# A hybrid sequence-mixing block on one Trainium2 core: the first two SwiGLU tiles in token halves, and the late modulation as one stream

## The chip, the core and the metric

The kernel runs on one core of one Trainium2 chip. A core has a matrix engine (TensorE, PE in the profile; its weight loads are PEld), three engines for element-wise work (VectorE or DVE, ScalarE or ACT, GpSimd or POOL) and SyncE (SP), which here issues transfers. Each engine works through its own instructions in order. An instruction waits at the head of its engine until the semaphores that it needs have been raised, and what stands behind it waits too. Transfers run on 16 DMA engines; they are issued by SP, ACT and POOL.

The metric is the device time of the whole kernel in microseconds (us), from the runs of it, taken as a median. A profile is one execution that the hardware profiler recorded; its times count from the start of its span.

## The reference

One layer of a diffusion backbone on 512 latent tokens (D = 1024) with 256 context tokens in front of them, in float32. The lines that the change touches are these:

```python
m_lat = (jax.nn.silu(c) @ mod_w[layer] + mod_b[layer])[:, None, :]
sh1, sc1, g1, sh2, sc2, g2 = jnp.split(m_lat, 6, axis=-1)
...
def swiglu(h, w_in, w_out):
    gate, up = jnp.split(h @ w_in, 2, axis=-1)
    return (jax.nn.silu(gate) * up) @ w_out
```

The conditioning vector `c` gives six rows of 1024, the modulation: shift, scale and gate of the first norm and mixers, and the same three for the second norm and the SwiGLU. `mod_w` is 1024 x 6144. The first normed and modulated input goes through one projection into two token mixers, a gated delta rule and HGRN2 (each with 4 heads, both directions). Their outputs are gated, projected up, merged and projected to D; times `g1` that is added to the input. The sum `x1` is normed again (RMSNorm, times 1 + `sc2`, plus `sh2`) and goes through the SwiGLU with 2816 features; times `g2` that is added to `x1`, and a last RMSNorm with the weight `final_norm_g` gives the output.

## The kernel before, in words

**Products.** A float32 product is made of three products of float32r operands: each operand is split into a high part and the rest (`hi`, `lo`), and TensorE adds hi.hi, lo.hi and hi.lo in PSUM (`mm3`, L100; the matmul is L105). Weights come through `split` (L84): SP issues the transfer of a 512 KB block `raw` (L92), ScalarE casts it to `hi` (L95), VectorE subtracts to get `lo` (L97). A tile of a pool has a number of buffers; a new tile of the same tag takes the buffer of an old one and waits until the old one's last reader is done. `raw`, `hi` and `lo` have two buffers each in the pool `wf`.

**Order.** The program is written in Python loops, and a scheduler puts each engine's instructions in an order by priority and by what is ready in its estimate; the waits follow from the tiles' readers and writers. So the order on an engine is not simply the order of the code.

**The modulation.** Sections 0 and 1 (first norm) are made at the start. The later sections are made in quarters of 256 columns: a weighted sum over 1024 rows of `mod_w`, in VectorE multiply-adds with the scalar `sc[:, k]`, and a sum over the partitions by two matmuls of one column (`mod_sum`, L843, matmul L846). Seven of the twelve quarters of the sections 2, 3 and 4 are made early, within the delta rule (`mod_early`, L830: transfer of 1 MB into a buffer of the delta rule that is not in use yet, multiplies L837 and L839). The other five (3,3 and 4,0 to 4,3, as section and quarter) are made behind it, and the four of section 5 in the SwiGLU, both by `mod_quarter` (L811): a generator that clears an accumulator (L815), loads half a quarter, 512 KB, by a transfer that GpSimd issues (L819) into one of two buffers, and multiplies it in four steps (L821). One such half is a step; `mods` holds the generators, and `mod_steps(n)` runs n steps. In the trace the halves are all called `mwb`; in the program they have numbers, section, quarter and first row block: `mwb330` is section 3, quarter 3, rows from block 0, `mwb334` its other half. The five quarters behind the delta rule are emitted at once (L915 to L922, ten transfers); those of the SwiGLU come one half to a feature tile, for tiles 3 to 12 (L1056, eight transfers).

**Behind the delta rule** run the rest of the HGRN2 heads (tiles `h_...`: VectorE's L464 and L465, ScalarE's copy L444, TensorE's L448), then merge and up-projection, output projection, and the second norm (L1010 to L1030), which works in two halves of the tokens: TensorE transposes into `px` (L1022), ScalarE and VectorE write the normed input as `hhi` and `hlo` (L1029, L1030). Each of these holds 8 blocks of 128 features by 512 tokens.

**SwiGLU** (L1033 to L1060). For each of 22 feature tiles f: two splits, of the gate's and the up part's weights (L1044); two PSUM banks `pf` (L1045); gate and up products, each 24 matmuls of 128 x 128 by 512 tokens. Tile 0 alone is done in two halves of the tokens, each 2 x 24 matmuls by 256 tokens (L1046), so that it can begin when the first half of the second norm is ready. Then sigmoid on ScalarE (L1051), two products on VectorE (L1052, L1053), and the split of the result into `uh` and `ul` (L1054, L1055). At f = 15 the modulation's section 5 is summed and spread over the partitions into `g2b`. The row `final_norm_g` is loaded to every partition (`fgb`, 512 KB, L1039, by GpSimd) ahead of the loop. The products with `w_out` follow (L1061 onwards), in two halves of the output columns; `g2b` and `fgb` are read behind them.

Of the kernel before, what the change touches and what calls it, by code (L numbers as in the profile page):

```python
# [7 lines left out]
F32 = mybir.dt.float32  # L8
F32R = mybir.dt.float32r
U8 = mybir.dt.uint8  # L10
AF = mybir.ActivationFunctionType
ALU = mybir.AluOpType

P = 128
D = 1024
KT = 8
# [13 lines left out]
# The order in which the streams of the mixers are emitted: name and number of steps; X ends the delta rule.  # L30
# [13 lines left out]
def view(ap, offset, dims):  # L44
    """The tile behind ap, all partitions, with free dimensions given as (step, count)."""
    return bass.AP(ap.tensor, ap.offset + offset, [list(ap.ap[0])] + [list(d) for d in dims])


def body(tc, T, out, tap=None):
# [8 lines left out]
    with ExitStack() as root:  # L58
# [25 lines left out]
        def split(srcs, kt, n, pool=None):  # L84
            """Loads [kt * 128, n] of weights side by side and splits them into two float32r parts."""
            WN[0] += 1
            pool = pool or ring["w"]
            raw = pool.tile([P, kt, n], F32, name=f"raw{WN[0]}", tag="raw", bufs=2)
# [5 lines left out]
            hi = pool.tile([P, kt, n], F32R, name=f"hi{WN[0]}", tag="hi")  # L94
            nc.scalar.copy(hi[:, :, :], raw[:, :, :])  # L95
            lo = pool.tile([P, kt, n], F32R, name=f"lo{WN[0]}", tag="lo")
# [3 lines left out]
        def mm3(ps, a, b, kt, start=True, stop=True):  # L100
            """ps += sum_k a_k^T b_k with a, b as (hi, lo) callables of k."""
# [6 lines left out]
        def feat(w, src, n, name, t0=0, tag="mm"):  # L108
            """[128 features, n tokens from t0] of the projection with the weights w."""
# [22 lines left out]
        def gate_low(i, pool):  # L132
            """The same in two halves of the features, out of its own buffers."""
# [15 lines left out]
        with ExitStack() as st:  # L149
# [4 lines left out]
            # small vectors, one row of 128 to a partition: those of the first norm, then the others  # L154
# [71 lines left out]
            def sigmoid_small(dst, src):  # L226
                """1 / (1 + exp(-src)), for the small tiles."""
# [25 lines left out]
            def modulation(d, s):  # L253
                """Shift and scale columns of feature tile d, for the latents (s = 0) or the context (s = 1)."""
# [12 lines left out]
            def mod_columns(s, d0, d1):  # L267
                """The columns of the feature tiles d0 to d1, with the biases and the weight of the norm."""
# [144 lines left out]
        def head_norm(po, gcol, i, on, y, ss, tag, name, eq=None):  # L413
            """po: [128 tokens, 4, 128] -> normalised, scaled by the channel weight, transposed, spilled as row i of ydram."""
# [396 lines left out]
        def mod_quarter(sec, j):  # L811
# [12 lines left out]
            def finish():  # L824
                mod_sum(sec, j, acc, "mm")
# [291 lines left out]
```

## Time and profile before

| what | value |
| --- | --- |
| three runs | 1109.54, 1112.13, 1111.83 us; median 1111.83 |
| profiled execution: span | 1115.9 us, 4.07 above the median |
| mean granted clock of TensorE | 0.980 |
| delta rule and all before it, 0 to 540 us | TensorE busy 500.05 of 540.00 |
| HGRN2 tail, merge, output projection, second norm, 540 to 735 us | TensorE busy 184.41 of 195.00 |
| SwiGLU, gate and up products, 735 to 911 us | TensorE busy 173.61 of 176.00 |
| `w_out` products and the last norm, 911 us to the end | TensorE busy 195.94 of 204.90 |

The profiled execution's own time is known as its span; no other time of it was taken. A row of a timeline gives the start and the duration in us, the engine, the line of the kernel, the operation, the tile written and the tiles read (their numbers left out), the number of instructions put together in the row and, in brackets, how long the engine stood idle before it and what ended that. Matmuls overlap, so a matmul's duration is longer than the distance to the next; paces are taken from starts.

### The profile page before, as it was taken

The page shows a single profiled execution, that of the slowest core. Times are in us where ns is not written, and L with a number is a line of the kernel's source. Part 1 is how long each engine was busy: PE and PEld are TensorE (multiplying, and loading weights), DVE is VectorE, ACT ScalarE, POOL GpSimd, SP SyncE. Part 2 cuts the span into 40 slices and gives each one's busy share as a digit, 9 for nine tenths or more (in the row PEclk, how much of TensorE's full clock was granted, in tenths as well). Part 3 has the DMA queues.
Part 4 walks back from the last instruction along what each step waited for, and adds up shares of the span by engine and source line. Part 5 has one row for each costly group of instructions (what it writes and reads, how often), then busy time and mean ns, then how long its engine had stood idle before and what let it go on. Part 6 is the DMA issues. An engine that isn't in the chain of part 4 may idle for free.

```text
span 1115.9 us, 15740 instructions
## 1 busy us (share of the span) xinstructions
PE 1054.0 (94%) x6007; PEld 879.1 (79%) x6007; DVE 696.8 (62%) x1365; ACT 560.1 (50%) x1062; POOL 75.8 (7%) x132
## 2 busy tenths in 40 slices
PE   4999999979999999999988999899999999999996
PEld 3787788858897887799777887787888888888785
DVE  5896877679676868866796675586343433422424
ACT  3454568747886765887764743452222222221212
POOL 0010000220001022000201000010000000000000
PEclk9998999989999999999999999999999999999999
DMA  9943322222003213200637853455333332322222
GB/s 303 283 149 109 114 76 57 58 76 57 3 20 114 76 48 86 57 2 11 194 118 227 299 153 123 129 167 159 93 93 94 94 88 80 93 94 94 92 95 94
DMA packets 142720, 122.02 MB, mean 109 GB/s; under 512 B 5534, under 2 KB 118452, under 8 KB 142644
## 3 DMA queue, kind: packets, MB, share of 16 engines
q1 hardware_dynamic: 135907, 100.20, 30.1%
q0 software_dynamic: 4640, 17.30, 4.8%
q10 hardware_dynamic: 2096, 3.50, 1.0%
q8 instruction: 47, 0.77, 0.3%
q14 instruction: 30, 0.24, 0.1%
HBM read 110.51 MB, written 10.49 MB: 108 GB/s over the span
## 4 chain that ended last, share of the span: by engine, by line
PE 57%; DVE 10%; issue 5%; ACT 3%; POOL 2%; DMA 2%; POOLq 0%; ACTq 0%; DVEq 0%
PE pf L105 19%; PE pfo L105 10%; PE pgate L105 4%; PE pup L105 4%; PE pwo L105 3%; PE h_z L105 2%; DMA mwb<-in_mod_w_dram 2%; PE h_pA L477 2%; PE h_zv L105 1%; DVE lo L97 1%; PE p_s_pk L778 1%; PE p_s_pk L787 1%; DVE p_o L683 1%; PE p_s_pk L775 1%; DVE p_Z L685 1%
## 5 line engine op out<-in xcount | busy, mean ns | idle before, releaser
L95 ACT CAST hi<-raw 128x1024 fp32r<-128x1024 f32 (+1 forms) x137 | 135.7, 991 | 307.4 <-PE pf L105 131.2
L97 DVE TENSOR_TENSOR lo<-raw,hi 128x1024 fp32r<-128x1024 f32 (+1 forms) x137 | 157.9, 1152 | 177.5 <-ACT hi L95 176.9
L105 PE MATMUL pf<-hhi,lo 128*128 128x512 f32 (+1 forms) x368 | 142.9, 389 | 2.4 <-DVE lo L97 2.4
L105 PE MATMUL pf<-hlo,hi 128*128 128x512 f32 (+1 forms) x368 | 143.0, 390 | 0.7 <-DVE hlo L1030 0.7
L105 PE MATMUL pf<-hhi,hi 128*128 128x512 f32 (+1 forms) x368 | 142.4, 390 | 0.0
L105 PEld LDWEIGHTS pf<-hhi,lo 128*128 128x128 f32 x368 | 69.8, 190 | 18.5 <-DVE lo L97 3.3
L105 PEld LDWEIGHTS pf<-hlo,hi 128*128 128x128 f32 x368 | 69.7, 190 | 16.5 <-DVE hlo L1030 1.1
L105 PEld LDWEIGHTS pf<-hhi,hi 128*128 128x128 f32 x368 | 69.7, 190 | 15.1
L105 PE MATMUL pfo<-lo,uh 128*128 128x512 f32 x176 | 69.8, 396 | 0.1
L105 PE MATMUL pfo<-hi,ul 128*128 128x512 f32 x176 | 69.5, 395 | 0.0
L105 PE MATMUL pfo<-hi,uh 128*128 128x512 f32 x176 | 68.7, 395 | 0.0
L105 PE MATMUL pgate<-hhi,lo 128*128 128x512 f32 x144 | 60.6, 422 | 6.7 <-DVE lo L97 6.7
L105 PE MATMUL pgate<-hhi,hi 128*128 128x512 f32 x144 | 61.1, 424 | 1.8 <-ACT hi L95 1.8
L105 PE MATMUL pgate<-hlo,hi 128*128 128x512 f32 x144 | 59.8, 416 | 0.0
L1053 DVE TENSOR_TENSOR sg<-sg,pf 128x512 f32<-128x512 f32 x22 | 15.1, 688 | 53.2 <-PE pf L105 53.2
L821 DVE SCALAR_TENSOR_TENSOR acc<-mwb,sc,acc 128x256 f32<-128x256 f32 x72 | 34.3, 482 | 13.0 <-DMA mwb<-in_mod_w_dram 11.7
L261 DVE SCALAR_TENSOR_TENSOR macc<-mw,sc,macc 128x256 f32<-128x256 f32 x96 | 40.0, 479 | 0.0
L105 PEld LDWEIGHTS pfo<-lo,uh 128*128 128x128 f32 x176 | 33.1, 188 | 8.7 <-DVE lo L97 1.0
L105 PEld LDWEIGHTS pgate<-hhi,lo 128*128 128x128 f32 x144 | 28.5, 198 | 14.4 <-DVE lo L97 9.2
L105 PE MATMUL h_z<-hhi,hi 128*128 128x512 f32 x96 | 39.3, 410 | 0.3 <-ACT abT L365 0.3
L105 PE MATMUL h_z<-hlo,hi 128*128 128x512 f32 x96 | 39.4, 411 | 0.0
L105 PEld LDWEIGHTS pfo<-hi,uh 128*128 128x128 f32 x176 | 32.9, 188 | 8.2 <-ACT hi L95 0.6
(422 smaller groups left out, 2566.3 us busy)
## 6 DMA issues: line engine op xcount, KB each, us to landing
raw<-in_ffn_w_in_dram SPq DMA_DIRECT2D x44, 512.0 KB, 3.9
raw<-in_w_in_dram SPq DMA_DIRECT2D x37, 512.0 KB, 3.9
raw<-in_ffn_w_out_dram SPq DMA_DIRECT2D x22, 512.0 KB, 3.5
mwb<-in_mod_w_dram POOLq DMA_DIRECT2D x18, 512.0 KB, 4.9
mw<-in_mod_w_dram SPq DMA_DIRECT2D x16, 512.0 KB, 6.3
mwe<-in_mod_w_dram POOLq DMA_DIRECT2D x7, 1024.0 KB, 6.2
gdram<-gt SPq DMA_DIRECT2D x24, 256.0 KB, 2.4
raw<-in_w_in_dram SPq DMA_DIRECT2D x18, 256.0 KB, 3.0
```

The source lines that it names most:

```text
L95: nc.scalar.copy(hi[:, :, :], raw[:, :, :])
L97: nc.vector.tensor_tensor(lo[:, :, :], raw[:, :, :], hi.bitcast(F32), op=ALU.subtract)
L105: nc.tensor.matmul(ps, a[u](k), b[v](k), start=(start and n == 0), stop=(stop and n == tot - 1))
L261: nc.vector.scalar_tensor_tensor(acc[:, :], mws[d][:, k, :], col, acc[:, :], op0=ALU.mult, op1=ALU.add)
L477: nc.tensor.matmul(pA[:, P * c:P * c + P], kq[:, 0, P * c:P * c + P], kq[:, 1, P * c:P * c + P], start=True, stop=True)
L683: nc.vector.tensor_tensor(ov, Z[:, r + 1:32, r:r + 1].to_broadcast([P, 31 - r, r]), Z[:, r:r + 1, 0:r].to_broadcast([P, 31 - r, r]), op=AL ...
L685: nc.vector.tensor_tensor(Z[:, r + 1:32, 0:r], Z[:, r + 1:32, 0:r], ov, op=ALU.add)
L775: nc.tensor.matmul(pk[:, 0:P], KTt[:, g, :], S[t][:, :], start=True, stop=True)
L778: nc.tensor.matmul(pk[:, P:2 * P], N[:, d, e, g, :], rt[:, :], start=True, stop=True)
L787: nc.tensor.matmul(pk[:, 2 * P:3 * P], kend[:, :], u[:, :], start=True, stop=True)
L821: nc.vector.scalar_tensor_tensor(acc[:, :], mw[:, k - k0, :], sc[:, k:k + 1], acc[:, :], op0=ALU.mult, op1=ALU.add)
L1053: nc.vector.tensor_tensor(sg[:, :], sg[:, :], pgu[1][:, :], op=ALU.mult)
```

## The change

It has three parts.

1. `split` can take its `hi` and `lo` from another pool with a number of buffers given. The weights of tile 0 come from `wf` as before, those of tile 1 get buffers of their own in the pool `ff`. Tiles 0 and 1 are both done in two halves of the tokens, in the order half 0 of tile 0, half 0 of tile 1, half 1 of tile 0, half 1 of tile 1. `g2b` and `fgb` later use these buffers, so the load of `fgb` is emitted behind the two tiles.
2. The late modulation is one generator over all halves of all quarters (`mod_quarters`). It allocates and loads the buffer of step i + 1 before the multiplies of step i.
3. The first multiply of a quarter writes the accumulator (TENSOR_SCALAR, L835) instead of adding to it, and the clearing goes.

The diff, without the comments that it also removes:

```diff
-        def split(srcs, kt, n, pool=None):
+        def split(srcs, kt, n, pool=None, bufs=None):
...
-            raw = pool.tile([P, kt, n], F32, name=f"raw{WN[0]}", tag="raw", bufs=2)
+            raw = (ring["w"] if bufs else pool).tile([P, kt, n], F32, name=f"raw{WN[0]}", tag="raw", bufs=2)
...
-            hi = pool.tile([P, kt, n], F32R, name=f"hi{WN[0]}", tag="hi")
+            hi = pool.tile([P, kt, n], F32R, name=f"hi{WN[0]}", tag="hi", bufs=bufs)
...
-        def mod_quarter(sec, j):
+        def mod_quarters(qs):
             mp = ring["mod"]
-            acc = mp.tile([P, 256], F32, name=f"acc{sec}{j}", tag="acc", bufs=12 if sec < 5 else 4)
-            nc.vector.memset(acc[:, :], 0.0)
-            for k0 in range(0, KT, MK):
-                mw = mp.tile([P, MK, 256], F32, name=f"mwb{sec}{j}{k0}", tag="mw", bufs=2)
-                c0 = D * sec + 256 * j
-                nc.gpsimd.dma_start(mw[:, :, :], T["mod_w"][0, P * k0:P * k0 + MK * P, c0:c0 + 256].rearrange("(k p) f -> p k f", p=P))
+            steps = [(sec, j, k0) for sec, j in qs for k0 in range(0, KT, MK)]
+            tiles = {}
+
+            def load(i):
+                if i < len(steps):
+                    sec, j, k0 = steps[i]
+                    tiles[i] = mp.tile([P, MK, 256], F32, name=f"mwb{sec}{j}{k0}", tag="mw", bufs=2)
+                    c0 = D * sec + 256 * j
+                    nc.gpsimd.dma_start(tiles[i][:, :, :],
+                                        T["mod_w"][0, P * k0:P * k0 + MK * P, c0:c0 + 256].rearrange("(k p) f -> p k f", p=P))
+
+            load(0)
+            for i, (sec, j, k0) in enumerate(steps):
+                load(i + 1)
+                if k0 == 0:
+                    acc = mp.tile([P, 256], F32, name=f"acc{sec}{j}", tag="acc", bufs=12 if sec < 5 else 4)
+                    late.append(lambda sec=sec, j=j, acc=acc: mod_sum(sec, j, acc, "mm"))
+                mw = tiles.pop(i)
                 for k in range(k0, k0 + MK):
-                    nc.vector.scalar_tensor_tensor(acc[:, :], mw[:, k - k0, :], sc[:, k:k + 1], acc[:, :], op0=ALU.mult, op1=ALU.add)
+                    if k == 0:
+                        nc.vector.tensor_scalar_mul(acc[:, :], mw[:, 0, :], sc[:, 0:1])
+                    else:
+                        nc.vector.scalar_tensor_tensor(acc[:, :], mw[:, k - k0, :], sc[:, k:k + 1], acc[:, :], op0=ALU.mult, op1=ALU.add)
                 yield
...
-        mods += [mod_quarter(*q) for q in quarters]
+        mods.append(mod_quarters(quarters))
...
-            g2b = ff.tile([P, D], F32, name="g2b", bufs=1)
-            fgb = ff.tile([P, D], F32, name="fgb", bufs=1)
-            nc.gpsimd.dma_start(fgb[:, :], T["final_norm_g"].unsqueeze(0).to_broadcast([P, D]))
...
-            mods += [mod_quarter(5, j) for j in range(4)]
+            mods.append(mod_quarters([(5, j) for j in range(4)]))
+            pgus = {}
+
+            def ffn_in(f, wss, t0, n):
+                if f not in pgus:
+                    pgus[f] = [bank(("mm", "ha")[f % 2], f"pf{f}_{j}") for j in range(2)]
+                for j in range(2):
+                    mm3(pgus[f][j][:, t0:t0 + n], [lambda k, t=t: t[:, k, :] for t in wss[j]],
+                        [lambda k, t=t: t[:, k, t0:t0 + n] for t in lat], KT)
+
+            def ffn_weights(f, **kw):
+                return [split([W[:, o + P * f:o + P * f + P]], KT, P, **kw) for o in (0, DFF)]
+
+            w01 = ffn_weights(0), ffn_weights(1, pool=ff, bufs=2)
+            for t0 in (0, 256):
+                for f in range(2):
+                    ffn_in(f, w01[f], t0, 256)
+            g2b = ff.tile([P, D], F32, name="g2b", tag="hi", bufs=2)
+            fgb = ff.tile([P, D], F32, name="fgb", tag="lo", bufs=2)
+            nc.gpsimd.dma_start(fgb[:, :], T["final_norm_g"].unsqueeze(0).to_broadcast([P, D]))
             for f in range(NF):
-                ws = [split([W[:, o + P * f:o + P * f + P]], KT, P) for o in (0, DFF)]
-                pgu = [bank(("mm", "ha")[f % 2], f"pf{f}_{j}") for j in range(2)]
-                for t0, n in ((0, 256), (256, 256)) if f == 0 else ((0, SEQ),):
-                    for j in range(2):
-                        mm3(pgu[j][:, t0:t0 + n], [lambda k, t=t: t[:, k, :] for t in ws[j]],
-                            [lambda k, t=t: t[:, k, t0:t0 + n] for t in lat], KT)
+                if f > 1:
+                    ffn_in(f, ffn_weights(f), 0, SEQ)
+                pgu = pgus[f]
```

In the orders below, `hi` and `lo` carry the number of the weight block: 74 and 75 are gate and up part of tile 0, 76 and 77 of tile 1, 80 and 81 of tile 3. `pf1_0` is the gate bank of tile 1, `pf0_1` the up bank of tile 0, and so on; the number behind the last underscore only tells one buffer from another.

TensorE at the end of tile 0, before:

```order
L105 MATMUL pf0_1_7080<-hhi_73,hi75_7075 128x256
L105 MATMUL pf0_1_7080<-hlo_74,hi75_7075 128x256
L105 MATMUL pf0_1_7080<-hhi_73,lo75_7077 128x256
L105 MATMUL pf1_0_7195<-hhi_73,hi76_7185 128x512
L105 MATMUL pf1_0_7195<-hlo_74,hi76_7185 128x512
L105 MATMUL pf1_0_7195<-hhi_73,lo76_7187 128x512
```

TensorE at the same place, after:

```order
L105 MATMUL pf1_0_7133<-hhi_73,hi76_7073 128x256
L105 MATMUL pf1_0_7133<-hlo_74,hi76_7073 128x256
L105 MATMUL pf0_1_7084<-hlo_74,hi75_7067 128x256
L105 MATMUL pf0_1_7084<-hhi_73,lo75_7069 128x256
L105 MATMUL pf0_1_7084<-hhi_73,hi75_7067 128x256
L105 MATMUL pf0_1_7084<-hlo_74,hi75_7067 128x256
L105 MATMUL pf0_1_7084<-hhi_73,lo75_7069 128x256
L105 MATMUL pf1_1_7134<-hhi_73,hi77_7079 128x256
L105 MATMUL pf1_1_7134<-hlo_74,hi77_7079 128x256
L105 MATMUL pf1_0_7133<-hhi_73,lo76_7075 128x256
```

Tile 1 now comes in matmuls of 256 tokens. Apart from the first two of its gate, all of them stand behind tile 0, the second token half of tile 0 included: the scheduler has not kept the interleaving of the code.

VectorE between the gate's and the up part's split of tile 3, before:

```order
L97 TENSOR_TENSOR lo80_7323<-raw80_7319,hi80_7321 128x1024
L1052 TENSOR_TENSOR sg2_7313<-sg2_7313,pf2_0_7263 128x512
L821 SCALAR_TENSOR_TENSOR acc52_7687<-mwb524_7763,sc_173,acc52_7687 128x256 x4
L821 SCALAR_TENSOR_TENSOR acc53_7837<-mwb530_7839,sc_173,acc53_7837 128x256
L1053 TENSOR_TENSOR sg2_7313<-sg2_7313,pf2_1_7264 128x512
L821 SCALAR_TENSOR_TENSOR acc53_7837<-mwb530_7839,sc_173,acc53_7837 128x256
L97 TENSOR_TENSOR lo81_7329<-raw81_7325,hi81_7327 128x1024
```

VectorE at the same place, after:

```order
L97 TENSOR_TENSOR lo80_7366<-raw80_7362,hi80_7364 128x1024
L1076 TENSOR_TENSOR sg2_7356<-sg2_7356,pf2_0_7306 128x512
L837 SCALAR_TENSOR_TENSOR acc52_7732<-mwb524_7730,sc_173,acc52_7732 128x256 x3
L835 TENSOR_SCALAR acc53_7881<-mwb530_7805,sc_173 128x256
L837 SCALAR_TENSOR_TENSOR acc52_7732<-mwb524_7730,sc_173,acc52_7732 128x256
L837 SCALAR_TENSOR_TENSOR acc53_7881<-mwb530_7805,sc_173,acc53_7881 128x256 x2
L1077 TENSOR_TENSOR sg2_7356<-sg2_7356,pf2_1_7307 128x512
L837 SCALAR_TENSOR_TENSOR acc53_7881<-mwb530_7805,sc_173,acc53_7881 128x256
L97 TENSOR_TENSOR lo81_7372<-raw81_7368,hi81_7370 128x1024
```

Three multiplies and the TENSOR_SCALAR of `mwb530` now stand ahead of the up part's split where two multiplies stood, and the first of them stands ahead of the last multiply of `mwb524`.

GpSimd's transfers in the SwiGLU, before, from the load of `fgb` on:

```order
L1039 DMA fgb_7065<-in_final_norm_g_dram 128x1024
L819 DMA mwb500_7389<-in_mod_w_dram 128x4x256
L819 DMA mwb504_7463<-in_mod_w_dram 128x4x256
L819 DMA mwb510_7539<-in_mod_w_dram 128x4x256
L819 DMA mwb514_7613<-in_mod_w_dram 128x4x256
```

GpSimd after:

```order
L823 DMA mwb500_7430<-in_mod_w_dram 128x4x256
L823 DMA mwb504_7432<-in_mod_w_dram 128x4x256
L823 DMA mwb510_7507<-in_mod_w_dram 128x4x256
L1069 DMA fgb_7280<-in_final_norm_g_dram 128x1024
L823 DMA mwb514_7581<-in_mod_w_dram 128x4x256
```

The load of `fgb` has moved from ahead of the eight transfers to behind the third. Its buffer is one of tile 1's, and it waits for the last matmul of tile 1's gate. The order of the ten transfers behind the delta rule is unchanged on this queue, but since the buffers are now allocated ahead of the accumulator, the first two (`mwb330`, `mwb334`) lie in the memory of the early quarter `mwe32` and wait for its sum (the last L846 of the early quarters), where before it was `mwe31`, the quarter ahead of it. SP's order of weight loads is the same before and after.

5 lines of the change are left out of this document (1 added, 4 removed).

## The prediction

> **What bounds the kernel now.** I read the page first, then TensorE's waits, the chain that ended last, the timelines around the waits, and the table of windows. From the page:
>
> ```profile
> span 1115.9 us, 15740 instructions
> ...
> PE 57%; DVE 10%; issue 5%; ACT 3%; POOL 2%; DMA 2%; POOLq 0%; ACTq 0%; DVEq 0%
> ```
>
> More than half of the chain that sets the end is TensorE's. Other engines matter where TensorE waits for them. TensorE's waits from 540 us to the end (columns: total us, times, longest):
>
> ```profile
> PE px L1022 <- ACT hhi L1029: 2.8, 2, 2.5
> PE pf L105 <- DVE lo L97: 2.4, 2, 2.0
> PE h__pt L426 <- ACT h_on L423: 2.1, 1, 2.1
> PE h_pv L448 <- ACT h_Zv L444: 2.0, 1, 2.0
> ```
>
> The row of `pf` is where the change works: 2.4 us in two waits, 0.40 for the second feature tile's weights (quoted further down) and 2.0 for the fourth tile's up weights. VectorE and GpSimd (start, duration, operation, idle before and its releaser) ahead of the longer one:
>
> ```profile
> 767.02 0.48 DVE L821 SCALAR_TENSOR_TENSOR acc<-mwb,sc,acc 128x256 f32<-128x256 f32 x1 [2.39 <-DMA mwb<-in_mod_w_dram]
> 767.42 0.68 DVE L1053 TENSOR_TENSOR sg<-sg,pf 128x512 f32<-128x512 f32 x1
> 768.02 0.48 DVE L821 SCALAR_TENSOR_TENSOR acc<-mwb,sc,acc 128x256 f32<-128x256 f32 x1
> 768.42 1.22 DVE L97 TENSOR_TENSOR lo<-raw,hi 128x1024 fp32r<-128x1024 f32 x1
> ```
>
> ```profile
> 759.62 0.77 POOL L819 DMA_DIRECT2D mwb<-in_mod_w_dram  x1 [0.67 <-issue]
> ```
>
> And how long the eight transfers of this stage took to land (the tile mwb, 724 to 775 us):
>
> ```profile
> DMA to landing us min/median/max: 4.2/5.1/7.4
> ```
>
> The transfer issued at 759.62 (mwb530: section 5, quarter 3, first rows) was multiplied only from 767.02, 7.4 us later: it is the slowest of the eight. Behind its first multiply in VectorE's order stand a gate product, another multiply and the split that TensorE needs. Then TensorE:
>
> ```profile
> 767.30 0.40 PE L105 MATMUL pf<-hlo,hi 128*128 128x512 f32 x1
> 769.69 0.50 PE L105 MATMUL pf<-hhi,lo 128*128 128x512 f32 x1 [2.00 <-DVE lo L97]
> ...
> 771.32 0.63 PE L105 MATMUL pf<-hhi,lo 128*128 128x512 f32 x1
> ...
> 773.88 0.63 PE L105 MATMUL pf<-hhi,lo 128*128 128x512 f32 x1
> ```
>
> From 771.32 to 773.88 six matmuls take 2.56 us, 0.427 each; the usual pace stands below, 0.2325. The reason is in the windows (stretch; us; PE, PEld, DVE, ACT, POOL busy with instructions; granted clock; DMA share; GB/s):
>
> ```profile
> 716.40:719.80 3.40, 2.37 (x14) 1.77 (x12) 3.34 (x5) 2.25 (x4) 0.00 (x0) 1.00 0.00 0
> 719.80:723.20 3.40, 1.61 (x12) 1.41 (x12) 3.37 (x7) 3.36 (x8) 0.00 (x0) 1.00 0.54 154
> 767.60:771.00 3.40, 1.41 (x7) 1.09 (x7) 3.36 (x6) 2.06 (x3) 0.00 (x0) 1.00 0.20 75
> 771.00:774.40 3.40, 3.40 (x10) 2.62 (x9) 3.26 (x7) 0.00 (x0) 0.00 (x0) 0.50 0.49 145
> ```
>
> TensorE is busy 1.41 of 3.40 us in the window with the wait, and the window behind it runs at clock 0.50. So the stall has a second price: 3.40 x (1 - 0.2325/0.427) = 1.55 us. The waits of 2.5 us for `px` are spread over two windows (busy 2.37 and 1.61) and no halving follows. After the wait the chain is TensorE alone:
>
> ```profile
> 769.69 141.35 PE pf L105 x598
> ```
>
> None of the four waits lies behind that row, so what is gained before 769.69 reaches the end whole.
>
> **Part 1: two tiles in token halves.** The first tile is halved in the kernel before too; new is that the second is. TensorE at the seam of both, and what the split waits for:
>
> ```profile
> 737.09 0.28 PE L105 MATMUL pf<-hhi,hi 128*128 128x256 f32 x1
> ...
> 738.39 0.28 PE L105 MATMUL pf<-hhi,lo 128*128 128x256 f32 x1
> 738.51 0.39 PE L105 MATMUL pf<-hhi,hi 128*128 128x512 f32 x1
> ...
> 739.53 0.50 PE L105 MATMUL pf<-hhi,lo 128*128 128x512 f32 x1 [0.40 <-DVE lo L97]
> 739.87 0.39 PE L105 MATMUL pf<-hhi,hi 128*128 128x512 f32 x1
> ```
>
> ```profile
> 737.17 1.05 ACT L95 CAST hi<-raw 128x1024 fp32r<-128x1024 f32 x1 [0.93 <-PE pf L105]
> ```
>
> Eleven half-wide steps take 738.39 - 737.09 = 1.30 us, 0.118 each (11.35 for 96); from 739.87 to 767.30 lie 118 full ones, 27.43 us, 0.2325 each. Before, the second tile's last 45 matmuls run from 739.87 and the third tile starts at 739.87 + 45 x 0.2325 = 750.33. After, the cast no longer waits 0.93 us for a buffer that TensorE still reads, since this tile has its own; the cast can start at 737.17 - 0.93 = 736.24 and the split is done at 736.24 + 1.05 + 1.22 = 738.5, when TensorE arrives, and 96 half-wide matmuls from 738.51 end at 738.51 + 11.35 = 749.86. That is **-0.47**: the 0.40 us wait goes, and the halves cost nothing I can separate (96 x 0.118 against 48 x 0.2325 is +0.19, against two slow matmuls at the seam). Interleaving itself gives nothing else: in the new order only the second tile's gate stands, for two products, among the last matmuls of the first tile, behind its second token half, so it covers none of the wait for that half's norm. Cast (1.05) and split (1.22) are covered by the first tile's 48 half-wide matmuls of the second token half, 48 x 0.118 = 5.7 us; were that cover gone, the 0.40 would be back.
>
> **Part 2: the late modulation as one stream.** "A step ahead" starts no transfer earlier by itself: GpSimd issued each as soon as its buffer was free, and the order of transfers is unchanged. What does change: nine multiplies become TENSOR_SCALARs and nine memsets go. VectorE's price of the former, from the early quarters:
>
> ```profile
> 541.38 0.61 DVE L837 TENSOR_SCALAR mwe<-mwe,sc 128x256 f32<-128x256 f32 x2 [0.95 <-DMA mwe<-in_mod_w_dram]
> ```
>
> 0.30 each against 0.48 (the multiplies quoted above). In the SwiGLU stage I follow VectorE's new order from 738.5 with 1.2 for a split, 0.6 from one gate product to the next instruction, 0.30 and 0.48 for the multiplies and 5.1 from issue to landing. Split, gate product, first multiply, gate product, two multiplies, product, multiply: mwb500 is done and mwb510 issued at 743.3. It lands at 748.4, its first multiply stands ahead of the last of mwb504, so mwb514 is issued at 748.4 + 0.30 + 0.48 = 749.2; mwb520 after three more multiplies and a gate product, 751.2; mwb524 at 749.2 + 5.1 + 1.9 = 756.2; mwb530 at 751.2 + 5.1 + 0.30 + 1.44 = 758.1 instead of 759.62. Between its landing and the split's end lie, in the new order, 0.30 + 0.45 + 0.95 + 0.60 + 0.45 + 1.22 = 4.0 us. TensorE wants the split at 749.86 + 74 x 0.2325 = 767.07. Landing after 4.2 us: ready at 766.3, no stall; after 5.1: 767.2, stall 0.1; after 7.4, as before: 769.5, stall 2.4. I take the median, so 0.1 of stall is left. The stall then gives 1.9 and, as its window holds no 2 us of idle time any more, the clock 1.55: **-3.45** against the profiled execution.
>
> The Trainium skill, "TensorE: Matmul & The Clock Gate", Part 1 (The HAM clock gate), puts the half clock behind a window of about 3.4 us that is idle as a whole, in windows that run freely. The trace does not agree on the first: 1.99 us idle were enough here. By the page's rule no halving would belong to this stall and its removal would be worth 2.0 at most.
>
> The fgb load (L1039) moves behind the third transfer and waits for the second tile's gate, 738.51 + 72 x 0.118 = 747.0. It is read only behind the first half of the SwiGLU's output products, so its own landing costs nothing; what queues behind it on GpSimd is mwb514, whose buffer comes free later, at 749.2, anyway. The stream's sums, g2b in a reused buffer: nothing, for the same reason.
>
> **Part 3: the stage behind the delta rule.** The first two late transfers take the memory of another early quarter than before. TensorE's sums of the two, and what follows on the late transfers:
>
> ```profile
> 543.94 0.50 PE L846 MATMUL pmo<-ones,mwe 128*128 128x1 f32 x4
> 545.34 0.50 PE L846 MATMUL pmo<-ones,mwe 128*128 128x1 f32 x4
> ```
>
> ```profile
> 552.57 0.48 DVE L821 SCALAR_TENSOR_TENSOR acc<-mwb,sc,acc 128x256 f32<-128x256 f32 x1 [2.20 <-DMA mwb<-in_mod_w_dram]
> 552.97 0.95 DVE L465 SCALAR_TENSOR_TENSOR h_sg<-h_Z,h_sg 128x768 f32<-128x768 f32 x1
> ...
> 562.39 0.33 PE L448 MATMUL h_pv<-sq,h_Zv 128*128 128x128 f32 x1 [1.95 <-ACT h_Zv L444]
> ```
>
> Issue is 545.34 - 543.94 = 1.40 us later. VectorE's `h_sg` stands right behind the first multiply, and through ScalarE leads to the `h_pv` wait. Passed on whole that is +1.40 less 0.18 for the cheaper first product, +1.2; if a later start meets quieter DMA engines and lands as before, -0.2 to -0.3. I take **+0.5**, near the middle.
>
> **The sum.** -0.47 - 3.45 + 0.5 = -3.4 against the span of 1115.9. But the three runs (1109.54, 1111.83, 1112.13) lie 4.1 below it in the median and 2.6 apart: part of these stalls is not in every execution. I count half of the stall and clock: -0.47 - 1.73 + 0.5 = -1.70, so 1111.83 - 1.70 = **1110.1**. A measurement of this kernel can tell about 0.3%, 3.3 us, from no change.
>
> **The rivals.**
> *A, the forecast, 0.51*: 1110.1, own range 1108.0 to 1112.0 by stage 1's bounds and the other half of the stall; of it 0.06 faster and 0.01 slower beyond 0.3%.
> *B, whole gain, 0.23*: the stall and its half clock stand in all runs and both go, and part 3 costs nothing: 1111.83 - 0.47 - 3.45 = 1107.9. For it: the wait's chain is in program order, not chance. Against: the runs are faster than the profiled execution. 0.20 beyond 0.3%.
> *C, the stall only moves, 0.15*: mwb530 lands 7.4 us behind its issue again, since a weight load takes its share of the DMA engines; stall 2.4 instead of 2.0 and the half clock stays: -0.47 + 0.5 + 0.4 = +0.4, 1112.3; 0.01 slower beyond 0.3%.
> *D, slower, 0.11*: the fgb load, now among the stream's transfers from 747.0 on, stretches those on the GpSimd queue. If mwb514 and mwb530 both take the 7.4 us that mwb530 took, mwb530 is issued 2.3 later and the split is ready at 758.1 + 2.3 + 7.4 + 4.0 = 771.8, a stall of 4.7 instead of 2.0, with its half clock: -0.47 + 0.5 + 2.7 = +2.7, 1114.6, and 1115.3 with part 3 at its upper bound. It ends above before once the two together land 1.9 us later than I assumed. Against: the fgb load is issued 2 us ahead of mwb514 and has the size of one of them, where before it lay beside the first two. 0.06 beyond 0.3%.
>
> The Trainium skill, "DMA: Bandwidth & Descriptors", on issuing engines that are not separate queues, has transfers of all issuers share the same engines and interleave; that speaks for C and D. The 7.4 us against a median of 5.1 agrees, without showing which transfer took the share.
>
> **The numbers.** Faster 0.06 + 0.20 = 0.26, slower 0.01 + 0.01 + 0.06 = 0.08, the same 0.66. The range from 1106.9 (B with part 3 at its lower bound and the runs' spread) to 1113.8 leaves out most of D and B's end.
>
> **What would show it.** Right: no PE wait on `lo` above 0.5 us after 738, no clock of 0.50 between 767 and 778, mwb530 issued near 758.1, the third tile starting 0.5 earlier against the second norm, and the `h_pv` wait 0 to 1.2 longer. Wrong: a PE wait of 2 us or more on the split of any tile up to the eighth (C, D), PE waiting on `hlo` of the second half, or a start of the SwiGLU stage, measured from the span's start, that is over 1.5 us off, which would put the result into part 3 or outside my parts.

## The result and the profile after

The changed kernel took 1117.51 us in the median of four runs (1115.65 to 1118.43), the kernel before 1110.68 in four (1108.07 to 1112.13). The ratio is 1.0052, with a 95% interval of 1.0029 to 1.0074: slower, by 6.8 us in the medians and 5.8 by the ratio, and outside the range of the prediction. Two runs in a slow state, 1294.81 us of the kernel before and 2608.54 of the halves alone, are left out of the ratios and of what follows.

The profiled execution of the changed kernel has a span of 1116.7 us and took 1118.43 as a run, so about 1.7 us lie around the span. From its page, the span and the engines' shares of the chain that ended last:

```profile
span 1116.7 us, 15827 instructions
...
PE 56%; DVE 9%; issue 6%; ACT 4%; DMA 3%; POOL 2%; POOLq 0%; ACTq 0%; DVEq 0%
```

By the two spans (1115.9 and 1116.7) hardly anything happened; by the runs 6 to 7 us did. With 1.7 us around it, the profiled execution of the kernel before took about 1117.6, an estimate. That is slower than each of its runs in all the comparisons below (the highest is 1116.95). The profile on which the prediction was built is real, but not typical.

TensorE's waits in the changed kernel, from 540 us (total, times, longest):

```profile
PE px L1033 <- ACT hhi L1040: 2.9, 2, 2.5
PE h__pt L426 <- ACT h_on L423: 2.4, 1, 2.4
PE h_pv L448 <- ACT h_Zv L444: 2.1, 1, 2.1
PE pf L105 <- DVE lo L97: 1.7, 1, 1.7
```

The 0.40 us wait of tile 1 is gone (`pf` now waits once). The wait of tile 3 is not: 1.7 us. Both waits behind the delta rule are longer (2.1 and 2.0 before). GpSimd and VectorE ahead of tile 3's wait:

```profile
751.54 0.55 POOL L1069 DMA_DIRECT2D fgb<-in_final_norm_g_dram  x1 [3.91 <-issue]
752.11 0.78 POOL L823 DMA_DIRECT2D mwb<-in_mod_w_dram  x1
...
763.34 0.77 POOL L823 DMA_DIRECT2D mwb<-in_mod_w_dram  x1 [1.58 <-DVE acc L837]
```

```profile
758.66 2.05 DVE L837 SCALAR_TENSOR_TENSOR acc<-mwb,sc,acc 128x256 f32<-128x256 f32 x4 [2.70 <-DMA mwb<-in_mod_w_dram]
760.63 0.35 DVE L835 TENSOR_SCALAR acc<-mwb,sc 128x256 f32<-128x256 f32 x1
761.01 1.53 DVE L837 SCALAR_TENSOR_TENSOR acc<-mwb,sc,acc 128x256 f32<-128x256 f32 x3
...
768.90 0.35 DVE L835 TENSOR_SCALAR acc<-mwb,sc 128x256 f32<-128x256 f32 x1 [2.37 <-DMA mwb<-in_mod_w_dram]
769.17 1.39 DVE L837 SCALAR_TENSOR_TENSOR acc<-mwb,sc,acc 128x256 f32<-128x256 f32 x3
770.48 0.68 DVE L1077 TENSOR_TENSOR sg<-sg,pf 128x512 f32<-128x512 f32 x1
771.08 0.48 DVE L837 SCALAR_TENSOR_TENSOR acc<-mwb,sc,acc 128x256 f32<-128x256 f32 x1
771.47 1.22 DVE L97 TENSOR_TENSOR lo<-raw,hi 128x1024 fp32r<-128x1024 f32 x1
```

The load of `fgb` now goes out directly ahead of mwb514 (752.11), which is multiplied 6.55 us later, at 758.66. The multiplies of mwb520 (760.63, 761.01) come right behind it and end at 762.54; mwb530, which takes their buffer, is issued 0.8 us after that, at 763.34, and multiplied from 768.90. All four of its multiplies stand ahead of the up part's split (768.90, two of the three at 769.17, and 771.08), where the kernel before had two.

Tile 1 itself: the 97th half-wide matmul begins at 742.19, and tile 2 at 753.69.

```profile
742.19 0.27 PE L105 MATMUL pf<-hlo,hi 128*128 128x256 f32 x1
...
753.69 0.39 PE L105 MATMUL pf<-hhi,hi 128*128 128x512 f32 x1
```

That is 11.50 us, where the kernel before took 750.32 - 738.51 = 11.81.

### The profile page after: what moved, and what is told of

Same layout as the page of the kernel before. It is cut to its first block, busy times and chain, and to the rows that moved or that the text cites. A ratio compares the mean times of both kernels' runs of the same rounds, so it can differ in the third digit from the quotient of the medians.

```text
span 1116.7 us, 15827 instructions
## 1 busy us (share of the span) xinstructions
PE 1054.8 (94%) x6055; PEld 882.8 (79%) x6055; DVE 693.5 (62%) x1356; ACT 560.1 (50%) x1062; POOL 75.4 (7%) x132
## 4 chain that ended last, share of the span: by engine, by line
PE 56%; DVE 9%; issue 6%; ACT 4%; DMA 3%; POOL 2%; POOLq 0%; ACTq 0%; DVEq 0%
PE pf L105 20%; PE pfo L105 10%; PE pgate L105 4%; PE pup L105 4%; PE pwo L105 3%; DMA mwb<-in_mod_w_dram 2%; PE h_zv L105 1%; PE h_pA L477 1%; PE h_z L105 1%; DVE lo L97 1%; PE p_s_pk L778 1%; PE p_s_pk L787 1%; DVE p_o L683 1%; DVE p_Z L685 1%; PE p_s_pk L775 1%
## 5 line engine op out<-in xcount | busy, mean ns | idle before, releaser
L105 PEld LDWEIGHTS pf<-hhi,lo 128*128 128x128 f32 x384 | 72.5, 189 | 16.3 <-DVE lo L97 2.1
L105 PEld LDWEIGHTS pf<-hlo,hi 128*128 128x128 f32 x384 | 72.6, 189 | 15.3 <-DVE hlo L1041 1.1
L105 PEld LDWEIGHTS pf<-hhi,hi 128*128 128x128 f32 x384 | 72.3, 190 | 13.9
L105 PEld LDWEIGHTS pfo<-hi,ul 128*128 128x128 f32 x176 | 33.2, 188 | 7.6
```

The costliest lines, as they stand in the source:

```text
L105: nc.tensor.matmul(ps, a[u](k), b[v](k), start=(start and n == 0), stop=(stop and n == tot - 1))
```

## The experiments

Two questions: which part of the change costs the time, and by what mechanism. Theories H, S and T are stated in the first expectation; M, F and O came with the second group. In the diffs, only what differs from the kernel named is shown.

### The kernel before, once more

No edit. Expected:

> The kernel before once more. Theory H (the measured loss is made by windows of half clock that fall differently from execution to execution, in stages that the change does not touch): its runs scatter by some 5 us, and a profile near 1110 us has 3 to 4 half-clock windows fewer than the eleven that the first profile (span 1115.9) had before 1107 us. Theory S (the stream costs the time behind the delta rule) and theory T (the token halves cost it) both expect 1108 to 1112 and a profile whose stages beyond 540 us are as in the first one.

Measured: 1112.26 us in the median of 11 runs (1108.52 to 1114.70); ratio to the kernel before 0.9998 (0.9985 to 1.0012). The scatter is 6 us, and the profile, at 1113.37, has nine half-clock windows ahead of its last matmul where the first one had twelve (the expectation's eleven counts a double one once). Of the twelve and the nine, eight lie ahead of 540 us. Beyond 540 us the first profile has four (behind `h_pv`, `h__pt`, tile 3's wait, and the sums of section 5 at 911 us), this one a single one, behind `h__pt`. This much of H is right, and S and T's common expectation, that the stages beyond 540 us repeat, is wrong. TensorE's waits at `h_pv` and at tile 3 in this profile, and the windows around `h_pv`:

```profile
561.43 0.87 PE L448 MATMUL h_pv<-sq,h_Zv 128*128 128x128 f32 x6 [1.69 <-ACT h_Zv L444]
...
768.70 0.50 PE L105 MATMUL pf<-hhi,lo 128*128 128x512 f32 x1 [1.32 <-DVE lo L97]
```

```profile
558.70:562.10 3.40, 1.71 (x13) 1.23 (x12) 3.40 (x8) 1.39 (x4) 0.00 (x0) 1.00 0.79 246
562.10:565.50 3.40, 3.39 (x24) 2.65 (x23) 3.31 (x8) 2.91 (x6) 1.04 (x2) 1.00 0.43 148
```

The same two waits, 1.69 instead of 1.95 and 1.32 instead of 2.00, and no half clock behind either (at tile 3, TensorE is busy 2.08 of 3.40 in the window from 766.90 to 770.30, and the next is granted 1.00).

### The changed kernel, once more

No edit. Expected:

> The changed kernel once more, on the same chip. H: within 0.3% of the kernel before, either sign, with its profile's distance explained by the count of half-clock windows, about 1.5 us each. S and T: 5 to 8 us slower again.

Measured: 1117.31 us (1116.13 to 1118.84); ratio 1.0047 (1.0034 to 1.0061). So the loss is real, and H's expectation of no difference is wrong. This profile (span 1117.1) and the one above (span 1111.7) reach 540 us together, so all their difference of 5.4 us lies behind that. The changed kernel's row at 540 us, then the one before's:

```profile
540.22 0.33 PE L426 MATMUL p_pt<-sq,p_on 128*128 128x128 f32 x1 [0.83 <-ACT p_on L423]
```

```profile
540.26 0.33 PE L426 MATMUL p_pt<-sq,p_on 128*128 128x128 f32 x1 [0.84 <-ACT p_on L423]
```

The changed kernel's waits at `h_pv` and at tile 3, and its windows there:

```profile
562.28 0.88 PE L448 MATMUL h_pv<-sq,h_Zv 128*128 128x128 f32 x6 [2.58 <-ACT h_Zv L444]
...
770.92 0.51 PE L105 MATMUL pf<-hhi,lo 128*128 128x512 f32 x1 [2.75 <-DVE lo L97]
```

```profile
560.10:563.50 3.40, 1.11 (x7) 0.80 (x7) 3.40 (x9) 1.40 (x3) 0.75 (x1) 1.00 0.63 183
563.50:566.90 3.40, 3.24 (x15) 3.24 (x16) 2.03 (x4) 2.55 (x6) 0.75 (x1) 0.51 0.56 181
768.30:771.70 3.40, 0.78 (x3) 0.67 (x4) 3.16 (x5) 2.06 (x3) 0.57 (x1) 1.00 0.47 155
771.80:775.20 3.40, 3.40 (x10) 2.66 (x9) 2.60 (x5) 0.00 (x0) 0.00 (x0) 0.50 0.55 155
```

`h_pv` waits 0.9 longer, and a half window follows (1.55, the prediction's price of one, taken over as an estimate); `h__pt` waits 0.35 longer (2.4 against 2.0); tile 3 waits 1.43 longer, with a half window behind it that the other profile has not (1.55). These are 5.8. A third new half window stands behind the sums of section 5 (about 1.4). Against that go 0.4 of tile 1's wait and two small waits, 0.7 at `h_pA` and 0.4 at `pup`, that only the other profile has. The sum is 5.7.

### Each part alone

The stream without the halves: `mod_quarters` put into the kernel before. The halves without the stream: `mod_quarter` put into the changed kernel.

```diff
-        mods += [mod_quarter(*q) for q in quarters]
+        mods.append(mod_quarters(quarters))
...
-            mods += [mod_quarter(5, j) for j in range(4)]
+            mods.append(mod_quarters([(5, j) for j in range(4)]))
```

> The kernel before with the late modulation as one stream (and TENSOR_SCALAR for the first multiply), without the token halves. S: 4 to 7 us slower than the kernel before, in the waits h_pv and h__pt and what follows them. T: within 1 us of before. H: within 0.3% of before, not separable.

> The changed kernel with the late modulation as in the kernel before: only the token halves of tiles 0 and 1, own buffers for the weights of tile 1, the fgb load moved. T: 4 to 7 us slower than before, between 735 and 775 us. S: 0.5 us faster than before. H: within 0.3%, not separable.

Measured: the stream alone 1115.33 us, ratio 1.0033 (1.0021 to 1.0045); the halves alone, ratio 1.0038 (1.0021 to 1.0055), about 4 us. Each part loses by itself, so S and T were each right that their part costs something (S's 4 us or more was a little too much) and wrong that the other costs nothing. In the profiles, the stream alone has `h_pv` waiting 2.1 and no wait at tile 3; the halves alone have 1.1 at `h_pv` and 3.0 at tile 3. T's place, between 735 and 775 us, is right for the halves.

### The stream with accumulators allocated first

To the stream alone, the accumulator's allocation is moved to its place in the kernel before, ahead of the load buffers:

```diff
                 if i < len(steps):
                     sec, j, k0 = steps[i]
+                    if k0 == 0:
+                        accs[sec, j] = mp.tile([P, 256], F32, name=f"acc{sec}{j}", tag="acc", bufs=12 if sec < 5 else 4)
...
-                    acc = mp.tile([P, 256], F32, name=f"acc{sec}{j}", tag="acc", bufs=12 if sec < 5 else 4)
+                    acc = accs[sec, j]
```

> The stream alone, as in the run of that name, but the accumulator of a quarter is allocated ahead of its two load buffers, as in the kernel before; then mwb330 and mwb334 lie in the memory of mwe31 again and wait for nothing else than before. Theory S (the later start of the first two late transfers costs the time behind the delta rule): the wait h_pv falls from 2.1-2.6 to 1.1-2.0 us, h__pt from 2.3-2.4 to 2.0-2.15, and the time from 1115.3 to within 1.5 us of the kernel before, or up to 2 us under it, since the stall of tile 3 stays away. Theory M (the stream costs it in the SwiGLU, or by chance of the clock windows): it stays at 1114 to 1117.

Measured: 1111.29 us, ratio 0.9985 (0.9967 to 1.0002), 4.0 us under the stream alone by the medians and 5.3 by the ratios (the two ran in different groups, each beside runs of the kernel before). S held in the time and at `h_pv`, which waits 1.4; `h__pt` stayed at 2.3 and tile 3 waits 1.0, both against S. The first late transfers and VectorE's row that waits for them, in the stream alone:

```profile
545.95 1.56 POOL L823 DMA_DIRECT2D mwb<-in_mod_w_dram  x2 [5.67 <-DVE vc L859]
```

```profile
552.65 0.35 DVE L835 TENSOR_SCALAR acc<-mwb,sc 128x256 f32<-128x256 f32 x1 [2.48 <-DMA mwb<-in_mod_w_dram]
552.92 0.96 DVE L465 SCALAR_TENSOR_TENSOR h_sg<-h_Z,h_sg 128x768 f32<-128x768 f32 x1
```

and with the accumulators first:

```profile
544.19 1.56 POOL L825 DMA_DIRECT2D mwb<-in_mod_w_dram  x2 [4.27 <-DVE vc L861]
```

```profile
551.58 0.35 DVE L837 TENSOR_SCALAR acc<-mwb,sc 128x256 f32<-128x256 f32 x1 [1.76 <-DMA mwb<-in_mod_w_dram]
551.85 0.95 DVE L465 SCALAR_TENSOR_TENSOR h_sg<-h_Z,h_sg 128x768 f32<-128x768 f32 x1
```

GpSimd waits 5.67 us instead of 4.27 for the buffer, the predicted 1.40; VectorE waits 2.48 instead of 1.76, with `h_sg` right behind. So 0.7 of the 1.40 comes through (the later transfer is also multiplied sooner after its issue, 6.70 us against 7.39), and it is the allocation order that does it: nothing else differs between the two kernels.

### The fgb load, and both undone

From the changed kernel, `fgb` gets a buffer of its own and its load goes back ahead of mwb500; `yt` shares the buffers of `sg` to make room. The second kernel has the allocation order of the last experiment as well.

```diff
+            fgb = ff.tile([P, D], F32, name="fgb", bufs=1)
+            nc.gpsimd.dma_start(fgb[:, :], T["final_norm_g"].unsqueeze(0).to_broadcast([P, D]))
             W = T["ffn_w_in"][0]
...
-            fgb = ff.tile([P, D], F32, name="fgb", tag="lo", bufs=2)
-            nc.gpsimd.dma_start(fgb[:, :], T["final_norm_g"].unsqueeze(0).to_broadcast([P, D]))
...
-                    t = ff.tile([P, 512], F32, name=f"yt{half}{g}", tag="yt")
+                    t = ff.tile([P, 512], F32, name=f"yt{half}{g}", tag="sg")
```

> The changed kernel with the load of fgb ahead of mwb500, into a buffer of its own, as in the kernel before (yt shares the buffers of sg to make room). Theory F (the fgb load, directly ahead of mwb514 on GpSimd's queue, stretches that transfer and so the chain to mwb530): mwb514 lands in 5.0 to 5.6 us instead of 6.85, mwb530 is issued 1 to 1.5 us earlier against the end of tile 1, the wait of pf on lo falls from 1.7-2.75 to 0.5-1.5 us and the time by 1.5 to 3 us. Theory O (the order of VectorE, three more multiplies ahead of the up part's split, and tile 1's halves cost it): the wait stays above 1.5 and the time within 1 us of 1117.3.

> The changed kernel with both: accumulators allocated first, fgb early. S and F: the two gains add up, 1110 to 1113, the kernel before's time or 1 us under it. M and O: still 1114 to 1118.

Measured: fgb early, 1116.66 us, ratio 1.0046 (1.0031 to 1.0061), not to be told from the changed kernel's 1117.31. mwb514 now takes 5.06 us (749.49 to 754.55), as F expected, and tile 3's wait is 1.5. F holds for the transfer and falls as far as the time goes. Both undone: 1114.70, ratio 1.0021 (1.0007 to 1.0035). The 2.0 us between them go with `h_pv`, which waits 1.1 instead of 2.2 and has no half window behind it; tile 3 still waits 2.0. This is what M and O expected in time, though the gain at `h_pv` speaks against M.

### Tile 1 in whole matmuls

From the kernel with both undone:

```diff
-            for t0 in (0, 256):
-                for f in range(2):
-                    ffn_in(f, w01[f], t0, 256)
+            for f, t0, n in ((0, 0, 256), (0, 256, 256), (1, 0, SEQ)):
+                ffn_in(f, w01[f], t0, n)
```

> The kernel of the run above with tile 1 in whole matmuls of 512 tokens (own buffers kept, tile 0 in halves as before). O: the three multiplies go behind the split of tile 3's up part, the wait of pf on lo falls under 1 us, and the time is 2 us or more under the run above. F: no stall worth 1 us in either; within 1 us of the run above. In both, if S holds, this is the fastest kernel, 1108 to 1111.

Measured: 1108.87 us, ratio 0.9978 (0.9962 to 0.9994): 5.8 us under the halves, and faster than the kernel before. No wait of `pf` on `lo` is left. VectorE at the place of tile 3's splits:

```profile
760.28 2.05 DVE L839 SCALAR_TENSOR_TENSOR acc<-mwb,sc,acc 128x256 f32<-128x256 f32 x4 [0.15 <-DMA mwb<-in_mod_w_dram]
762.25 0.68 DVE L1078 TENSOR_TENSOR sg<-sg,pf 128x512 f32<-128x512 f32 x1
762.85 1.22 DVE L97 TENSOR_TENSOR lo<-raw,hi 128x1024 fp32r<-128x1024 f32 x1
763.98 0.69 DVE L1080 TENSOR_TENSOR ul<-sg,uh 128x512 fp32r<-128x512 f32 x1
764.88 0.35 DVE L837 TENSOR_SCALAR acc<-mwb,sc 128x256 f32<-128x256 f32 x1 [0.21 <-DMA mwb<-in_mod_w_dram]
```

The split (762.85) now stands ahead of mwb530's multiplies (764.88 on). Nothing in the edit says so; with tile 1's matmuls whole, the scheduler puts the multiplies elsewhere. With own buffers, tile 1 takes 10.9 us whole (737.45 to 748.37 in TensorE's timeline) and 11.5 in halves.

### The same two without section 5

Do the halves cost anything beside the order that they bring about? One line leaves section 5 out of the two kernels above:

```diff
-            mods.append(mod_quarters([(5, j) for j in range(4)]))
```

> The kernel of e7_both_undone (stream with accumulators first, fgb early, tiles 0 and 1 in halves) without the modulation's section 5: its eight transfers and 32 multiplies in the SwiGLU are left out, the gate g2 is the bias alone. No transfer is waited for on VectorE behind 735 us. Theory O (the halves cost time only through the place that VectorE's order gives to mwb530): no wait of pf on lo, 2 to 5 us under e7_both_undone, 1109.5 to 1112.5, and 0.3 to 1 us above the run with tile 1 whole. Theory T (matmuls of 256 tokens, or two banks open at once, cost it themselves): 4 us or more above the run with tile 1 whole.

> The kernel of e8_tile1_whole, section 5 of the modulation left out in the same way. O: within 1 us of e8_tile1_whole, 1108 to 1110, since it has no stall to lose, and 0.3 to 1 us under the halves. T: 4 us or more under the halves.

Measured: halves 1108.20 us (ratio 0.9963, 0.9946 to 0.9980), whole 1107.62 (0.9955, 0.9938 to 0.9971). The difference of 0.6 is inside the intervals, and of the size of what whole matmuls save in tile 1. By the ratios (the two pairs ran in different groups) section 5 costs 0.0058, 6.4 us, in the kernel with halves, and 0.0023, 2.6 us, in the one with tile 1 whole; O had expected 2 to 5 and at most 1. Part of both is TensorE's own work, which O left out: with tile 1 whole, the sums and the spreading of `g2b` take 3.93 us (905.29 to 909.22), without section 5 the spreading alone 1.70 (904.57 to 906.27). Without these 2.2 us, section 5 costs about 4.2 us with the halves and 0.4 with tile 1 whole. So it is shown that the halves lose almost only together with section 5, not by themselves. That they lose through VectorE's order is read from the profiles, where TensorE waits for the split that stands behind mwb530's multiplies with the halves and not with tile 1 whole; no kernel here changes that order alone.

### Own buffers alone, and with the stream in the SwiGLU only

The kernel of e8_tile1_whole with the late modulation of the kernel before; then the same with the stream again for section 5 alone.

```diff
-        mods.append(mod_quarters(quarters))
+        mods += [mod_quarter(*q) for q in quarters]
...
-            mods.append(mod_quarters([(5, j) for j in range(4)]))
+            mods += [mod_quarter(5, j) for j in range(4)]
```

> The kernel before with own buffers for the weights of tile 1 and nothing else of the change: tile 1 in whole matmuls, the late modulation as before, fgb early, yt in the buffers of sg. In its order all multiplies of mwb530 stand behind the split of tile 3's up part. O: no wait of pf on lo above 0.5 us, neither for tile 1 nor for tile 3, h_pv and h__pt as before; 2 to 4 us under the kernel before, level with e8_tile1_whole within 1 us. T and F: 0.4 to 1 us under the kernel before, from tile 1's wait alone.

> The kernel of e8_tile1_whole with the late modulation behind the delta rule as in the kernel before (cleared accumulators, one generator to a quarter), and the stream for section 5 alone. It stands between e11_own_buffers_only (1112.28, ratio 1.0004) and e8_tile1_whole (1108.87, ratio 0.9978). If the 3.4 us between them come from the stage behind the delta rule (the cheaper first multiplies shorten h_pv): ratio 0.999 to 1.001 and h_pv waiting 1.5 to 1.8. If they come from the SwiGLU (mwb534's multiplies end earlier): ratio 0.997 to 0.9985, and no wait at tile 4. If it is neither, the ratio lies between.

Measured: own buffers alone 1112.28 us, ratio 1.0004 (0.9988 to 1.0019). O's expectation of a gain of 2 to 4 us fails here; the 0.4 to 1 us that T and F expected can't be told from none, as the interval reaches 1.3 us under the kernel before. Tile 1 and tile 3 do not wait, but a wait of 0.9 has appeared at the next split, of tile 4's gate, behind mwb534, so of the 1.7 us that `pf` waits in the second profile of before, 0.8 is won:

```profile
773.45 2.05 DVE L821 SCALAR_TENSOR_TENSOR acc<-mwb,sc,acc 128x256 f32<-128x256 f32 x4 [0.88 <-DMA mwb<-in_mod_w_dram]
775.41 1.22 DVE L97 TENSOR_TENSOR lo<-raw,hi 128x1024 fp32r<-128x1024 f32 x1
```

With the stream in the SwiGLU, 1109.12 us, ratio 0.9983 (0.9965 to 1.0000), no wait at tile 4, and 1.5 at `h_pv`. That lies where the SwiGLU was expected to be the place, but the intervals of the two kernels overlap, and the wait of 0.9 is less than the 2 to 3 us between them. How much of it is real stays open.

### The profiles side by side

What TensorE waited, and whether the window behind had half clock; and the time from the last `p_pt` transpose to the first `pup` matmul, read from TensorE's timeline:

| kernel | mwb330 in | h_pv | half | p_pt to pup | tile 3 | half |
| --- | --- | --- | --- | --- | --- | --- |
| before, first profile | mwe31 | 2.0 | yes | 82.0 | 2.0 | yes |
| before, second | mwe31 | 1.7 | no | 81.7 | 1.3 | no |
| halves only | mwe31 | 1.1 | no | 79.4 | 3.0 | yes |
| own buffers only | mwe31 | 1.8 | no | 80.1 | 0 | no |
| stream, acc first | mwe31 | 1.4 | no | 80.6 | 1.0 | no |
| both undone | mwe31 | 1.1 | no | 80.5 | 2.0 | yes |
| tile 1 whole | mwe31 | 0.8 | no | 80.0 | 0 | no |
| stream in SwiGLU only | mwe31 | 1.5 | no | 79.5 | 0 | no |
| stream only | mwe32 | 2.1 | yes | 82.8 | 0 | no |
| fgb early | mwe32 | 2.2 | yes | 82.6 | 1.5 | no |
| after, first | mwe32 | 2.1 | yes | 83.2 | 1.7 | no |
| after, second | mwe32 | 2.6 | yes | 83.6 | 2.8 | yes |

All four with the later buffer have the half window behind `h_pv`, one in eight of the others has. Their stretch is 83.0 us in the mean, that of the others 80.5. The half window behind `h__pt` lies in the same stretch: all four have it, and five of the other eight (both of before, acc first, both undone, tile 1 whole). Over these five the mean is 81.0, so 2.1 us go with the later buffer. Each row is one execution, and not always a typical one: those of halves only, stream only and fgb early are the fastest run of their kernel, those of after and of own buffers only the slowest. In these two columns, waits of 2.0 and more are followed by half clock, those of 1.8 and less are not. It is no sharp rule: at `h__pt` waits of 2.1 (halves only) and 2.3 (own buffers only) went without, so where a wait lies in the window counts too.

## Why the prediction was wrong

**Part 1 was right in mechanism, and 0.16 too large.** The 0.40 us wait went; tile 1 took 0.31 us less (0.47 predicted). The gain was in the buffers; the halves cost 0.6 of it, which I had put at 0.19 and set against the seam.

**Part 2 failed, at the step "I take the median, so 0.1 of stall is left".** The arithmetic ahead of it held in pieces: against the 97th matmul of the SwiGLU (738.51 before, 742.19 after), mwb510 goes out at 743.20 on the clock of before (743.3 predicted), and mwb514 at 748.43 (749.2). But mwb514 took 6.55 us, not the median of 5.1, so mwb520's multiplies, which stand behind its own, end 0.8 later (758.86 against 758.05); and 0.8 us lie between the last multiply and the issue that it frees, which I had left out. So mwb530 goes out at 759.66, not 758.1, and takes 5.56. From its first multiply to the split's end it is 3.8 us (768.90 to 772.69; 4.0 worked out), where the kernel before had 2.6 (767.02 to 769.64). The 7.4 us that I held for the risk did not come; the chain of transfers that wait for each other was costed with one median, and its bounds were tried on the last one only. So the stall and its half clock, counted as a gain of 1.73 in the sum, were not won: tile 3 waits 1.7 and 2.8 us in the two profiles of the changed kernel, against 2.0 and 1.3 in those of before. Rival D had the place, mwb514 behind `fgb`, but moving `fgb` back gave only 0.65 us, inside the noise, and left a wait of 1.5. The wait is gone in the kernels where mwb530's multiplies stand behind the split, or where there is no section 5. With two of the four ahead, as in the kernel before, the stream alone has no wait in its profile and the stream with accumulators first has 1.0.

**Part 3 was mis-sized, at the term "+0.5".** The later issue was right to the digit (1.40), and so was that a part only comes through: 0.7 at VectorE, 0.7 at `h_pv`, against +0.5. What I priced at nothing was the half window behind `h_pv`. It stood in the profile of before, so I took it as a thing that both kernels have. It is in one profile of eight with the old buffer in the table and in four of four with the new one. Undoing the buffer alone gave 4.0 us by the medians of the two stream kernels and 2.0 between the two with halves. The profiles of these pairs show 2.2 and 2.1 in that stage, against +0.5; what more the stream pair lost stays open.

**The sum's discount went the wrong way.** I saw that the runs lie 4 us below the profile and concluded that half of the gain is not there in most executions. The other half of that thought is missing: if the profile of before is a slow one, with the half windows already in it, then most executions of before have no such price to lose, and a change that lengthens a wait of 1.7 us may have one to pay. None of my rivals had that.

The loss, put together from the changed kernel downwards: 1117.31, less 0.65 (fgb early, not resolved), less 1.96 (accumulators first), less 5.83 (tile 1 whole) is 1108.87. The first of these steps crosses two groups of runs.

## What to carry to other kernels

Before trusting one profile, set its span beside the runs: a profile slower than all of them contains costs that the typical execution hasn't, and what a change does must be worked out for both. Where tiles are handed out by allocation order, moving an allocation moves what its first transfer waits for, so "issue a step ahead" can issue later. And when a scheduler orders a queue, look in the new order for what has come to stand ahead of the instruction that the busiest engine waits for: here the halves of tile 1, which brought four multiplies of a late transfer ahead of such a split, cost 5.8 us, and the wait that they were made for was 0.40.

## What the runs showed of the hardware

The clock of TensorE halves for about 3.4 us behind windows in which TensorE was partly busy, not only behind idle ones. In the windows above and in the prediction's, 1.41, 1.11 and 0.78 us busy of 3.40 led to it, 1.61 and 1.71 did not. That is no threshold: ahead of 540 us, in the first profile of before, a window with 1.86 us busy led to it too:

```profile
467.30:470.70 3.40, 1.86 (x45) 1.39 (x44) 3.40 (x4) 2.57 (x6) 0.74 (x1) 0.99 0.00 1
470.70:474.10 3.40, 3.40 (x22) 2.75 (x16) 0.75 (x2) 3.34 (x8) 0.00 (x0) 0.51 0.00 0
```

A window may even be busy and lead to it, when what fills it is small matmuls, a good part of them of one column, as with the sums of section 5 in the first profile of before:

```profile
910.86 1.62 PE L846 MATMUL pmo<-ones,acc 128*128 128x1 f32 x12
```

```profile
911.00:914.40 3.40, 3.33 (x29) 3.11 (x28) 3.24 (x8) 1.40 (x2) 0.00 (x0) 1.00 0.05 11
914.40:917.80 3.40, 3.40 (x12) 2.91 (x11) 0.95 (x2) 0.00 (x0) 0.00 (x0) 0.50 0.51 148
```

The second profile of the same kernel has no half window there: the windows do not start at the same place of the program in each execution. The wait for `px` shows it best. It is 2.46 to 2.48 us in all twelve profiles of the table. In three of them (halves only, own buffers only, both undone) most of it falls into one window, TensorE busy 1.15, 0.92 and 0.94 of 3.40, and a half window follows; in the nine others it is spread more evenly over two (1.5 us busy or more in each), and none follows. The Trainium skill, "TensorE: Matmul & The Clock Gate", Part 1, has the windows run freely, which these two profiles bear out, and asks for a window idle as a whole, which they do not.

Ahead of the last `p_pt` transpose all these kernels have the same instructions, yet up to 540 us their profiles have between 6 and 10 half-clock windows. That transpose starts at 540.07 us in the profile with 6 (halves only), and at 544.36 and 546.09 in the two with 10 (after, own buffers only). So 4 to 6 us between executions of the same code go with these windows, most of what the runs of one kernel scatter.
